# Turning gated features by VectorE and by way of memory, in a two-layer decoder trunk

## The chip, the cores and the metric

The kernel runs on one core of a Trainium2 chip. The metric is the device time of one execution in microseconds (us), lower is better. A core has several engines that run their own instruction streams in order and meet through semaphores: TensorE (PE, matrix products into PSUM; PEld is its loading of the stationary operand), VectorE (DVE), ScalarE (ACT), GpSimd (POOL) and SyncE (SP, which here only issues DMA transfers).

## The reference, cut to what matters

256 tokens, a model width of 1024, two layers. Each layer has a gated feed-forward block (FFN), a mixing block with two kinds of attention, a second FFN, and a per-layer embedding gate; so there are four FFNs, named a0, b0, a1 and b1 here (first and second FFN of layer 0 and of layer 1). All is float32.

```python
D_FF = 2816
def swiglu(x, w_gate, w_up, w_down):
    return (jax.nn.silu(x @ w_gate) * (x @ w_up)) @ w_down
...
    h = h + 0.5 * swiglu(rms_norm(h, ffn1_norm), ffn1_w_gate, ffn1_w_up, ffn1_w_down)
...
    h = h + 0.5 * swiglu(rms_norm(h, ffn2_norm), ffn2_w_gate, ffn2_w_up, ffn2_w_down)
```

The change concerns the tensor between the two halves of `swiglu`: the gated features, 256 tokens by 2816 features.

## The kernel before, in words

**Number form.** A float32 product is made of three products of a reduced form: every operand is split into a rounded high part and the rest (`wh` and `wl` for weights, `fh` and `fl` for gated features). ACT writes the high part (a copy that rounds), DVE subtracts it from the whole. `mm3` (L241) then issues three matmuls: high by high (L243), and two mixed ones, of which L244 reads `wl`.

**Weights.** A weight piece is 128 partitions by 1024 numbers (512 KB). SP loads it into one of 7 buffers `raw`, ACT makes `wh` (L139), DVE makes `wl` (L140); there are 8 buffers of each, so the splitting can be at most 8 pieces ahead of the product. Some blocks use seven products in place of eight (`Seven`, L161): there DVE also forms sums of raw weight pieces (L175), splits at L181, and ACT rounds at L180.

**FFN.** The 2816 features are worked in blocks of 512 (five) and one of 256, by `ffn` (L508). For a plain block the gate product `g` and the up product `u` are made for two halves of tokens (128 tokens each, t = 0 and 1), tokens on partitions: eight weight pieces. A block in `wide_sevens` is made by `wide_seven` (L547): first seven products of four weight pieces, then four more pieces. In a0 that is block 3 alone, in the other FFNs blocks 1 and 3. Then `gated` (L511) makes silu on ACT (`s`, L513) and the gated product on DVE (`pr`, L517), tokens on partitions.

**Turning.** The second half of the FFN needs the features on the partitions. `Gates.add` (L479) defers it: `go` has TensorE transpose the 128x512 tile in four 128x128 pieces into a PSUM bank (`ft`, L488), ACT rounds it into `fh` (L493) and DVE subtracts into `fl` (L494). For blocks 1, 2 and 3 `sums` (L435) also forms four sums of turned quarters, with an ACT copy (L451) and four subtractions or additions on DVE (L452 to L455), and splits them (L459, L460, L463, L464).

**Order.** `soon` (L222) puts a deferred piece into the program after so many us of estimated PE time, `flush` (L233) puts in all that are left. A scheduler then sets the order of each engine's instructions from its own estimates; each engine runs its list strictly in that order. SP's loads, ACT's roundings and DVE's splits of later weights are thus placed among the work on `pr`, `fh` and `fl`. Small work tiles come from tags `w0` to `w3` with two buffers each.

Of the kernel before, what the change touches and what calls it, by code (L numbers as in the profile page):

```python
# [9 lines left out]
F32 = mybir.dt.float32  # L10
# [7 lines left out]
P = 128  # L18
T = 256
# [33 lines left out]
def trunk(ctx: ExitStack, tc: tile.TileContext, xT, xr, pT, w, gains, fgain, consts, out):  # L53
# [218 lines left out]
    def wt(tag, name, n=2, width=T):  # L272

        return tp.tile([P, 768], F32, tag=tag, name=name)[:, : n * width].rearrange("p (a b) -> p a b", a=n)
# [4 lines left out]
    def half(f):  # L279
        return slice(f * 512, (f + 1) * 512)  # L280


    def split(x, src, c, gcol, name, ts=slice(0, T)):

# [130 lines left out]
    class Gates:  # L415
# [19 lines left out]
        def sums(self, i):  # L435

            a, b = self.turned[i, 0], self.turned[i, 1]
            lo, hi = slice(0, 2), slice(2, 4)
            e = SEVEN.index(i)
            if e == 0:  # L440

                self.spare = tuple(x_p.tile([P, KC, T], F32R, tag=f"x{q}", name=f"sx{q}_{self.tag}") for q in "hl")
            if e < 2:
                homes = [[q[:, 4 * e + k].rearrange("p (a b) -> p a b", a=2) for q in self.spare] for k in range(4)]
            else:

                homes = [[q[:, 2 + k].rearrange("p (a b) -> p a b", a=2) for q in self.tile(NBLK - 1)] for k in range(2)]
                homes += [[q[:, lo, P:T] for q in self.tile(b)] for b in SEVEN[:2]]
            two = [wt(f"w{2 + k}", f"sum{k}_{self.tag}_{i}") for k in range(2)]
            ss = s1, s2, s3, s4 = [two[k // 2][:, k % 2].rearrange("p (a b) -> p a b", a=2) for k in range(4)]  # L450
            nc.scalar.copy(s3, b[:, lo])  # L451
            nc.vector.tensor_tensor(s1, s3, b[:, hi], ALU.subtract)  # L452
            nc.vector.tensor_tensor(s2, s1, a[:, lo], ALU.subtract)
            nc.vector.tensor_tensor(s3, a[:, lo], s3, ALU.subtract)
            nc.vector.tensor_tensor(s4, s2, a[:, hi], ALU.add)  # L455
            if e < 2:
                for k in range(2):
                    sh, sl = (q[:, 4 * e + 2 * k : 4 * e + 2 * k + 2] for q in self.spare)
                    nc.scalar.activation(sh, two[k], AF.Copy)  # L459
                    nc.vector.tensor_tensor(sl, two[k], sh.bitcast(F32), ALU.subtract)  # L460
            else:
                for k, (sh, sl) in zip(ss, homes):
                    nc.scalar.activation(sh, k, AF.Copy)  # L463
                    nc.vector.tensor_tensor(sl, k, sh.bitcast(F32), ALU.subtract)  # L464
            self.s[i] = homes
# [12 lines left out]

        def add(self, i, t, pr, more):  # L479

            f = self.block(i)
            n = 4 if i < NBLK - 1 else 2

            def go():
                a = bank(f"ft_{self.tag}_{i}{t}")[:, : n * P]
                behind = newest_mm[0]
                for j in range(n):
                    after(nc.tensor.transpose(a[:, j * P : (j + 1) * P], pr[:, j * P : (j + 1) * P], ident), behind)  # L488
                a = a.rearrange("p (a b) -> p a b", a=n)

                ks = slice(2 if i in SEVEN and t else 0, n)
                fh, fl = both(f, slice(None), ks, slice(t * P, (t + 1) * P))
                nc.scalar.activation(fh, a[:, ks], AF.Copy)  # L493
                nc.vector.tensor_tensor(fl, a[:, ks], fh.bitcast(F32), ALU.subtract)  # L494
                self.turned[i, t] = a
                if i in SEVEN and t:
                    self.sums(i)

            soon(1.3 + 0.9 * t + more, go)

    def seven_mm(banks, x_of, ops, first, last):

# [5 lines left out]
    def ffn(x, n, tag, gcol, between=None, feed=None):  # L508
# [15 lines left out]
        def x_sums():  # L524

            v = f_p.tile([P, 4, T], F32, tag="f5h", name=f"xf_{tag}")
            xh, xl = (q[:, 0:4].bitcast(F32) for q in x)
            nc.vector.tensor_tensor(v, xh, xl, ALU.add)
            a11, a12, a21, a22 = (v[:, k : k + 2, t * P : (t + 1) * P] for t in range(2) for k in (0, 2))
            two = [wt(f"w{2 + k}", f"xsum{k}_{tag}") for k in range(2)]  # L530
            s1, s2, s3, s4 = (two[k // 2][:, k % 2].rearrange("p (a b) -> p a b", a=2) for k in range(4))
            nc.vector.tensor_tensor(s1, a21, a22, ALU.subtract)
            nc.vector.tensor_tensor(s2, s1, a11, ALU.subtract)
            nc.vector.tensor_tensor(s3, a11, a21, ALU.subtract)
            nc.vector.tensor_tensor(s4, s2, a12, ALU.add)
            xs.extend(f_p.tile([P, 4, T], F32R, tag=f"f4{q}", name=f"xs{q}_{tag}") for q in "hl")
            for k in range(2):
                sh, sl = (q[:, 2 * k : 2 * k + 2] for q in xs)
                nc.scalar.activation(sh, two[k], AF.Copy)
                nc.vector.tensor_tensor(sl, two[k], sh.bitcast(F32), ALU.subtract)  # L540
# [105 lines left out]

        head, tail = block(0), block(NBLK - 1)
        plain(head[:2], True)
        flush()

        p = {2: d[0][0], 3: d[0][1], 4: d[1][0]}
        p.update((i, bank(f"p{i}_{tag}")) for i in (1, 5, 6, 7))
        own = (1, 5, 6, 7)
        for i, c in zip(SEVEN, (head[2:], tail, [])):
            seven_mm(p, gates.seven(i), Seven().operands(), lambda q: q in own and i == SEVEN[0], lambda q: q in own and i == SEVEN[-1])
            plain(c)
            if i == SEVEN[1] and between is not None:
                between()
# [420 lines left out]
def _weights(i):  # L1079
# [9 lines left out]
    for L in range(DEPTH):  # L1089
# [5 lines left out]
        def ffn(n):  # L1095
            wg, wu, wd = (i[f"{n}_w_{s}"][L] for s in ("gate", "up", "down"))
            for j in range(NBLK - 1):
                m = ar(512 * j, 512 * j + 512)
                if j in wide_sevens(L == 0 and n == "ffn1"):
                    units.extend(np.concatenate([cols(v[k : k + 256], m) for v in (wg, wu)], axis=1) for k in (0, 256))  # L1100
                    units.extend(cols(v[512:], m) for v in (wg, wu))
                    continue
                wide(wg, m)
                wide(wu, m)
            m = ar(DFF - 256, DFF)
            wide(np.concatenate([wg[:, m], wu[:, m]], axis=1), ar(512))

            def down(b):
                units.extend(cols(wd[k : k + 256], ar(DM)) for k in range(512 * b, min(512 * b + 512, DFF), 256))

            def seven(b):
                for k in (512 * b, 512 * b + 256):
                    units.append(np.concatenate([cols(wd[k : k + 256], ar(c, c + 512)) for c in (0, 512)], axis=1))

            down(0)
            down(NBLK - 1)
            for b in SEVEN:
                seven(b)
            down(4)
# [81 lines left out]
```

## Time and profile before

| what | value |
|---|---|
| median of 3 executions | 1011.65 us (1010.78 to 1012.71) |
| profiled execution: time | 1010.68 us |
| profiled execution: span from first to last instruction | 1008.9 us |
| PE busy | 996.9 us (99%) |
| DVE busy | 839.9 us (83%) |
| ACT busy | 645.7 us (64%) |
| TensorE clock granted (mean) | 0.997 |
| DMA, mean over the span | 186 GB/s, 187.40 MB |

Times in rows are us from the start of the span unless they stand in a column of ns. The profile names tiles without their numbers: `wl` is any low part of a weight piece, `ft_a` a turned tile of a0 or a1, `ft_b` one of b0 or b1. `L488` is line 488 of the kernel. A matmul's row shows its whole passage, of which the next one's overlaps a part: how long PE is held by it is read from one start to the next. The same holds on DVE, where a row's time is a little longer than the step to the next start.

### The profile page before, as it was taken

To read this page: it belongs to the slowest core of one execution; us is meant where nothing else is said; L and a number is where in the kernel's file an instruction comes from. 1 tells how busy PE (TensorE), PEld (TensorE's weight loads), DVE (VectorE), ACT (ScalarE), POOL (GpSimd) and SP (SyncE) were. 2 spreads that over 40 slices of the span, in tenths; PEclk is the share of its full clock that TensorE was granted. 3 is DMA by queue.
4 is the path that set the end of the run, shared out by engine and by line. 5 is a ranking of instruction groups with operands and counts; after the bars stand their busy time and mean duration, and the time that the engine had idled before them with its cause. 6 is when DMAs were issued, how large, how long until landed. Compare 5 with 4: busy or idle time off the path is not lost.

```text
span 1008.9 us, 13852 instructions
## 1 busy us (share of the span) xinstructions
PE 996.9 (99%) x5064; PEld 842.3 (83%) x5064; DVE 839.9 (83%) x1170; ACT 645.7 (64%) x986; POOL 7.4 (1%) x13
## 2 busy tenths in 40 slices
PE   9999999999999999999999999999999999999996
PEld 8888888899888888888887888889998888888885
DVE  5799789966779987899998887899676898978994
ACT  5856566667566665657775665656766675656663
POOL 0000000000100000000000000000010000000000
PEclk9999999999999999999999999999999999999998
DMA  8947446674244566356637464557623364744641
GB/s 293 334 185 273 140 152 228 221 250 152 84 147 136 198 197 242 127 176 233 231 130 252 147 229 135 185 191 262 238 84 126 105 203 185 240 165 146 205 161 42
DMA packets 53492, 187.40 MB, mean 186 GB/s; under 512 B 6064, under 2 KB 6192, under 8 KB 53424
## 3 DMA queue, kind: packets, MB, share of 16 engines
q1 hardware_dynamic: 52992, 185.95, 54.1%
q8 instruction: 39, 0.64, 0.2%
q10 hardware_dynamic: 432, 0.57, 0.2%
q14 instruction: 29, 0.24, 0.1%
HBM read 185.45 MB, written 1.05 MB: 185 GB/s over the span
## 4 chain that ended last, share of the span: by engine, by line
PE 96%; ACT 1%; DVE 1%; DMA 1%; issue 1%; POOL 0%; DVEq 0%; ACTq 0%; POOLq 0%
PE p_b L243 3%; PE p_b L245 3%; PE p_b L244 3%; PE g_a L243 3%; PE g_a L245 3%; PE g_a L244 3%; PE g_b L245 3%; PE g_b L243 3%; PE g_b L244 3%; PE d_b L245 3%; PE d_b L244 3%; PE d_b L243 3%; PE u_a L244 3%; PE u_a L245 3%; PE u_a L243 3%; PE d_a L244 3%
## 5 line engine op out<-in xcount | busy, mean ns | idle before, releaser
L140 DVE TENSOR_TENSOR wl<-raw,wh 128x1024 fp32r<-128x1024 f32 (+1 forms) x278 | 324.5, 1191 | 59.3 <-ACT wh L139 58.8
L139 ACT ACTIVATE wh<-raw 128x1024 fp32r<-128x1024 f32 (+1 forms) x278 | 282.8, 1035 | 120.3 <-DMA raw<-in_w 14.4
L180 ACT ACTIVATE wh<-raw 128x1024 fp32r<-128x1024 f32 x133 | 139.6, 1060 | 123.2 <-DVE raw L175 58.7
L181 DVE TENSOR_TENSOR wl<-raw,wh 128x1024 fp32r<-128x1024 f32 x133 | 159.3, 1220 | 24.4 <-ACT wh L180 23.6
L175 DVE TENSOR_TENSOR raw<-raw,raw 128x1024 f32<-128x1024 f32 x76 | 92.7, 1219 | 14.9 <-DMA raw<-in_w 13.2
L243 PE MATMUL d_a<-wh,fh_a 128*128 128x512 f32 x108 | 42.7, 396 | 0.0
L243 PE MATMUL d_b<-wh,fh_b 128*128 128x512 f32 x108 | 42.7, 396 | 0.0
L245 PE MATMUL d_b<-wh,fl_b 128*128 128x512 f32 x108 | 42.1, 390 | 0.0
L245 PE MATMUL d_a<-wh,fl_a 128*128 128x512 f32 x108 | 42.1, 390 | 0.0
L244 PE MATMUL d_a<-wl,fh_a 128*128 128x512 f32 x108 | 42.1, 389 | 0.0
L244 PE MATMUL d_b<-wl,fh_b 128*128 128x512 f32 x108 | 42.1, 389 | 0.0
L243 PE MATMUL g_a<-wh,x0h 128*128 128x512 f32 x80 | 31.9, 401 | 0.0
L245 PE MATMUL g_a<-wh,x0l 128*128 128x512 f32 x80 | 31.0, 390 | 0.0
L244 PE MATMUL g_a<-wl,x0h 128*128 128x512 f32 x80 | 31.0, 390 | 0.0
L243 PE MATMUL g_b<-wh,x_mix0h 128*128 128x512 f32 x64 | 25.6, 400 | 0.0
L243 PE MATMUL g_b<-wh,x_mix1h 128*128 128x512 f32 x64 | 25.6, 400 | 0.0
L243 PE MATMUL g_a<-wh,xe0h 128*128 128x512 f32 x64 | 25.5, 401 | 0.0
L245 PE MATMUL g_a<-wh,xe0l 128*128 128x512 f32 x64 | 25.1, 392 | 0.0
L244 PE MATMUL u_a<-wl,x0h 128*128 128x512 f32 x64 | 25.0, 391 | 0.0
L245 PE MATMUL g_b<-wh,x_mix0l 128*128 128x512 f32 x64 | 25.0, 390 | 0.0
L245 PE MATMUL g_b<-wh,x_mix1l 128*128 128x512 f32 x64 | 25.0, 390 | 0.0
L244 PE MATMUL g_a<-wl,xe0h 128*128 128x512 f32 x64 | 25.0, 390 | 0.0
(556 smaller groups left out, 2702.2 us busy)
## 6 DMA issues: line engine op xcount, KB each, us to landing
raw<-in_w SPq DMA_DIRECT2D x338, 512.0 KB, 4.6
raw<-in_w SPq DMA_DIRECT2D x16, 256.0 KB, 4.6
xin<-in_xT SPq DMA_DIRECT2D x4, 256.0 KB, 5.1
h<-in_xr SPq DMA_DIRECT2D x2, 512.0 KB, 8.5
p<-in_pT SPq DMA_DIRECT2D x2, 256.0 KB, 4.8
fg<-in_fgain SPq DMA_DIRECT2D x1, 512.0 KB, 5.2
out_h<-hg SPq DMA_DIRECT2D x2, 256.0 KB, 2.3
out_h<-hg ACTq DMA_DIRECT2D x2, 256.0 KB, 2.7
```

The costliest lines, as they stand in the source:

```text
L139: nc.scalar.activation(wh[:, a], r[:, a], AF.Copy),
L140: nc.vector.tensor_tensor(wl[:, a], r[:, a], wh[:, a].bitcast(F32), ALU.subtract),
L175: nc.vector.tensor_tensor(self.raw[o], self.raw[a], self.raw[b], op)
L180: newest_wh[0] = nc.scalar.activation(wh, r, AF.Copy)
L181: nc.vector.tensor_tensor(wl, r, wh.bitcast(F32), ALU.subtract)
L243: nc.tensor.matmul(o, ah, bh, start=start, stop=False, **kw)
L244: nc.tensor.matmul(o, ah, bl, start=False, stop=False, **kw)
L245: newest_mm[0] = nc.tensor.matmul(o, al, bh, start=False, stop=stop, **kw)
```

## The change

The gated product `pr` is turned by one DVE instruction, in place, in blocks of 32 by 32 (tokens by features within each block). The turned tile is written to a buffer in memory (`m`, one DMA on SP), and four more DMAs on SP bring it back, 32 partitions each, so that every partition holds all tokens of its features (`ft`, now in a `w2` tile in SBUF, no longer in PSUM). Two estimates, `BACK` and `PARTS`, say when the DMAs back and the splitting stand in the program. The weight columns of gate and up are stored in another order, so that each feature lands on the partition that the down weights expect. In `sums` the ACT copy is gone (both sources are in SBUF), and its tiles come from `w3` alone. The first `flush` in the second half of the FFN stands behind the first seven products.

```diff
+BACK, PARTS = 2.5, 7.0
+def turned_order(n):
+    import numpy as np
+    return np.arange(n).reshape(n // P, 4, 32).transpose(1, 0, 2).reshape(-1)
...
+    mem_p = pool("mem", 4, space=bass.MemoryType.DRAM)
...
+    def in_runs(x):
+        return x.rearrange("p j (a s) -> p j a s", s=32)
...
-            two = [wt(f"w{2 + k}", f"sum{k}_{self.tag}_{i}") for k in range(2)]
-            ss = s1, s2, s3, s4 = [two[k // 2][:, k % 2].rearrange("p (a b) -> p a b", a=2) for k in range(4)]
-            nc.scalar.copy(s3, b[:, lo])
-            nc.vector.tensor_tensor(s1, s3, b[:, hi], ALU.subtract)
-            nc.vector.tensor_tensor(s2, s1, a[:, lo], ALU.subtract)
-            nc.vector.tensor_tensor(s3, a[:, lo], s3, ALU.subtract)
-            nc.vector.tensor_tensor(s4, s2, a[:, hi], ALU.add)
+            two = [wt("w3", f"sum{k}_{self.tag}_{i}") for k in range(2)]
+            ss = [two[k // 2][:, k % 2].rearrange("p (a b) -> p a b", a=2) for k in range(4)]
+            s1, s2, s3, s4 = (in_runs(s) for s in ss)
+            nc.vector.tensor_tensor(s1, b[lo], b[hi], ALU.subtract)
+            nc.vector.tensor_tensor(s2, s1, a[lo], ALU.subtract)
+            nc.vector.tensor_tensor(s3, a[lo], b[lo], ALU.subtract)
+            nc.vector.tensor_tensor(s4, s2, a[hi], ALU.add)
...
-            def go():
-                a = bank(f"ft_{self.tag}_{i}{t}")[:, : n * P]
-                behind = newest_mm[0]
-                for j in range(n):
-                    after(nc.tensor.transpose(a[:, j * P : (j + 1) * P], pr[:, j * P : (j + 1) * P], ident), behind)
-                a = a.rearrange("p (a b) -> p a b", a=n)
+            name = f"{self.tag}_{i}{t}"
+            nc.vector.transpose(pr, pr)
+            m = mem_p.tile([P, 4, n * 32], F32, tag="turn", name=f"m_{name}")
+            nc.sync.dma_start(m, pr.rearrange("p (q r) -> p q r", q=4))
+            a = wt("w2", f"ft_{name}", 4, n * 32)
+
+            def back():
+                for q in range(4):
+                    nc.sync.dma_start(a[32 * q : 32 * q + 32], m[:, q].rearrange("(a f) r -> f a r", a=4))
+
+            def parts():
+                self.turned[i, t] = v = a.rearrange("p a (j s) -> p j a s", j=n)
...
-                fh, fl = both(f, slice(None), ks, slice(t * P, (t + 1) * P))
-                nc.scalar.activation(fh, a[:, ks], AF.Copy)
-                nc.vector.tensor_tensor(fl, a[:, ks], fh.bitcast(F32), ALU.subtract)
-                self.turned[i, t] = a
+                fh, fl = (in_runs(q) for q in both(f, slice(None), ks, slice(t * P, (t + 1) * P)))
+                after(nc.scalar.activation(fh, v[:, ks], AF.Copy), newest_wh[0])
+                nc.vector.tensor_tensor(fl, v[:, ks], fh.bitcast(F32), ALU.subtract)
...
-            soon(1.3 + 0.9 * t + more, go)
+            soon(BACK, back)
+            soon(PARTS + t, parts)
...
-            two = [wt(f"w{2 + k}", f"xsum{k}_{tag}") for k in range(2)]
+            two = [wt("w3", f"xsum{k}_{tag}") for k in range(2)]
...
         plain(head[:2], True)
-        flush()
...
             seven_mm(p, gates.seven(i), Seven().operands(), lambda q: q in own and i == SEVEN[0], lambda q: q in own and i == SEVEN[-1])
+            flush()
...
-                m = ar(512 * j, 512 * j + 512)
+                m = 512 * j + turned_order(512)
...
-            m = ar(DFF - 256, DFF)
+            m = DFF - 256 + turned_order(256)
```

The order of instructions moves with it. On DVE in a0, at the end of block 2 (`pr_a0_20`, `pr_a0_21`) and the start of the wide block 3 (`raw7_12` and `wl7_12` are its four raw pieces and their splits; `wl14` is the first piece behind its seven products, `wl11` the last unit of block 2), the list before is:

```order
L181 TENSOR_TENSOR wl7_12_1_33_751<-raw7_12_1_745,wh7_12_1_33_750 128x1024
L540 TENSOR_TENSOR xsl_a0_714<-xsum1_a0_708,xsh_a0_713 128x512
L175 TENSOR_TENSOR raw7_12_0_725<-raw7_12_0_725,raw7_12_1_745 128x1024
L175 TENSOR_TENSOR raw7_12_1_745<-raw7_12_0_725,raw7_12_3_747 128x1024
L181 TENSOR_TENSOR wl7_12_0_34_780<-raw7_12_0_725,wh7_12_0_34_779 128x1024
L181 TENSOR_TENSOR wl7_12_1_35_793<-raw7_12_1_745,wh7_12_1_35_792 128x1024
L181 TENSOR_TENSOR wl7_12_2_36_806<-raw7_12_2_803,wh7_12_2_36_805 128x1024
L175 TENSOR_TENSOR raw7_12_0_725<-raw7_12_0_725,raw7_12_2_803 128x1024
L181 TENSOR_TENSOR wl7_12_0_37_817<-raw7_12_0_725,wh7_12_0_37_816 128x1024
L517 SCALAR_TENSOR_TENSOR pr_a0_20_699<-u_a0_20_522,hr_in_102,s_a0_20_623 128x512
L517 SCALAR_TENSOR_TENSOR pr_a0_21_703<-u_a0_21_523,hr_in_102,s_a0_21_625 128x512
L181 TENSOR_TENSOR wl7_12_3_38_827<-raw7_12_3_747,wh7_12_3_38_826 128x1024
```

And after the change, at the same place on DVE (two rows for the turning stand behind the gated products):

```order
L188 TENSOR_TENSOR raw7_12_1_759<-raw7_12_1_759,raw7_12_3_761 128x1024
L540 SCALAR_TENSOR_TENSOR pr_a0_20_712<-u_a0_20_538,hr_in_104,s_a0_20_636 128x512
L540 SCALAR_TENSOR_TENSOR pr_a0_21_720<-u_a0_21_539,hr_in_104,s_a0_21_638 128x512
L502 STREAM_TRANSPOSE pr_a0_20_712<-pr_a0_20_712 128x512
L502 STREAM_TRANSPOSE pr_a0_21_720<-pr_a0_21_720 128x512
L194 TENSOR_TENSOR wl7_12_1_33_765<-raw7_12_1_759,wh7_12_1_33_764 128x1024
L188 TENSOR_TENSOR raw7_12_0_746<-raw7_12_0_746,raw7_12_1_759 128x1024
L188 TENSOR_TENSOR raw7_12_1_759<-raw7_12_0_746,raw7_12_3_761 128x1024
L194 TENSOR_TENSOR wl7_12_0_34_784<-raw7_12_0_746,wh7_12_0_34_783 128x1024
L194 TENSOR_TENSOR wl7_12_1_35_797<-raw7_12_1_759,wh7_12_1_35_796 128x1024
L194 TENSOR_TENSOR wl7_12_2_36_810<-raw7_12_2_807,wh7_12_2_36_809 128x1024
```

Before, five of the seven splits stood ahead of the gated products of block 2; now one does, and the rest stands behind them. From `pr_a0_20` to the split of `wl14_0` the list now holds 10 instructions of 128x1024 (that split among them), 2 gated products, 2 turnings, 5 others of 128x512 and 5 of 128x256; before it held 2 of 128x1024, 2 gated products and 1 other of 128x512.

On SP in a0, the first block (`m_a0_00` and `m_a0_01` are the tiles in memory of the two token halves, `ft` the tiles that are brought back, the rest weight pieces), the list after is:

```order
L148 DMA raw8_0_0_24_542<-in_w 128x1024
L504 DMA m_a0_00_423<-pr_a0_00_418 128x512
L504 DMA m_a0_01_431<-pr_a0_01_428 128x512
L148 DMA raw8_1_0_25_568<-in_w 128x1024
L509 DMA ft_a0_00_425<-m_a0_00_423 32x4x128 x4
L509 DMA ft_a0_01_433<-m_a0_01_431 32x4x128 x4
L148 DMA raw9_0_0_26_586<-in_w 128x1024
L148 DMA raw9_1_0_27_620<-in_w 128x1024
L148 DMA raw10_0_0_28_642<-in_w 128x1024
L504 DMA m_a0_10_527<-pr_a0_10_522 128x512
L504 DMA m_a0_11_533<-pr_a0_11_530 128x512
L148 DMA raw10_1_0_29_660<-in_w 128x1024
```

Before, the same list held the weight pieces alone. Now the load of `raw8_1` stands behind two writes that wait for DVE, and that of `raw9_0` behind eight DMAs that wait for those writes to land.

## Rows read from the trace of the kernel before

**Rows 1.** The page: busy time by engine, with share of the span and instructions, and shares of the chain of work that ended last.

```profile
PE 996.9 (99%) x5064; PEld 842.3 (83%) x5064; DVE 839.9 (83%) x1170; ACT 645.7 (64%) x986; POOL 7.4 (1%) x13
...
PE 96%; ACT 1%; DVE 1%; DMA 1%; issue 1%; POOL 0%; DVEq 0%; ACTq 0%; POOLq 0%
```

**Rows 2.** Who waited for whom, PE alone: us in total, times, longest.

```profile
PE ft_a L488 <- DVE pr_a L517: 1.5, 1, 1.5
```

**Rows 3.** Windows over the four FFNs (a0, b0, a1, b1; each from its first product to near its last): length, then busy us of PE, PEld, DVE, ACT and POOL with the number of instructions, granted clock, DMA share, GB/s.

```profile
5.00:182.00 177.00, 177.00 (x802) 146.07 (x802) 150.82 (x189) 114.53 (x155) 0.00 (x0) 1.00 0.66 229
290.00:467.00 177.00, 177.00 (x808) 146.45 (x807) 155.89 (x195) 110.85 (x146) 0.00 (x0) 1.00 0.54 186
508.00:679.00 171.00, 169.53 (x768) 139.82 (x768) 147.38 (x177) 104.19 (x128) 0.00 (x0) 1.00 0.54 182
788.00:965.00 177.00, 177.00 (x807) 146.44 (x806) 155.98 (x196) 110.75 (x145) 0.00 (x0) 1.00 0.55 186
```

**Rows 4.** The transposes: the groups by source line (durations in ns), and PE's timeline around one group of four and one of two (start, time, instruction; in a start-to-start step PE is held).

```profile
L488 PE MATMUL ft_a<-c_sb,pr_a x88: 270/272/299, 45.3 to 630.2; 128*128 128x128 f32 x88
L488 PE MATMUL ft_b<-c_sb,pr_b x88: 270/272/273, 317.5 to 916.9; 128*128 128x128 f32 x88
...
45.08 0.39 PE L245 MATMUL u_a<-wh,x0l 128*128 128x512 f32 x1
45.31 0.60 PE L488 MATMUL ft_a<-c_sb,pr_a 128*128 128x128 f32 x4
45.67 0.47 PE L243 MATMUL u_a<-wh,x0h 128*128 128x512 f32 x1
45.98 0.39 PE L244 MATMUL u_a<-wl,x0h 128*128 128x512 f32 x1
...
417.41 0.38 PE L488 MATMUL ft_b<-c_sb,pr_b 128*128 128x128 f32 x2
417.54 0.48 PE L243 MATMUL d_b<-wh,fh_b 128*128 128x512 f32 x1
417.86 0.40 PE L244 MATMUL d_b<-wl,fh_b 128*128 128x512 f32 x1
```

**Rows 5.** DVE instructions from SBUF to SBUF, by source line (ns, smallest, median, largest): one source of 512 elements; and the groups by form of two sources, 512 and 1024 elements (busy us, mean ns).

```profile
L830 DVE TENSOR_SCALAR on_mla<-os,tss_mla x4: 480/486/489, 278.4 to 776.5; 128x512 f32<-128x512 f32 x4
...
L460 DVE TENSOR_TENSOR sxl_a<-sum_a,sxh_a 128x512 fp32r<-128x512 f32 x8 | 5.2, 686 | 0.2 <-ACT sxh_a L459 0.2
L140 DVE TENSOR_TENSOR wl<-raw,wh 128x1024 fp32r<-128x1024 f32 x262 | 314.1, 1222 | 53.0 <-ACT wh L139 52.5
```

**Rows 6.** DMA issues: size of one, and median us from issue to landing. The row of 64 KB is 128 runs of 512 bytes.

```profile
raw<-in_w SPq DMA_DIRECT2D x338, 512.0 KB, 4.6
out_h<-hg SPq DMA_DIRECT2D x2, 256.0 KB, 2.3
c_sb<-in_consts SPq DMA_DIRECT2D x1, 64.0 KB, 4.0
```

**Rows 7.** SP's timeline: issues at the start of a0 and before block 3.

```profile
18.25 0.44 SPq L1050 DMA_DIRECT2D h<-in_xr  x1
40.36 4.32 SPq L135 DMA_DIRECT2D raw<-in_w  x4
```

**Rows 8.** Timelines of DVE and PE in a0, block 0's gated products, the split behind them, and the first matmul that reads that split.

```profile
36.45 1.41 DVE L517 SCALAR_TENSOR_TENSOR pr_a<-u_a,hr_in,s_a 128x512 f32<-128x512 f32 x2 [1.46 <-ACT s_a L513]
37.98 1.23 DVE L140 TENSOR_TENSOR wl<-raw,wh 128x1024 fp32r<-128x1024 f32 x1
39.38 0.40 PE L244 MATMUL u_a<-wl,x0h 128*128 128x512 f32 x1
```

**Rows 9.** Timelines in a0 from block 1's gated products to block 3's first plain piece: DVE, then PE's first matmul that reads `wl14_0`.

```profile
51.12 1.40 DVE L517 SCALAR_TENSOR_TENSOR pr_a<-u_a,hr_in,s_a 128x512 f32<-128x512 f32 x2
...
64.43 2.48 DVE L175 TENSOR_TENSOR raw<-raw,raw 128x1024 f32<-128x1024 f32 x2
66.84 3.62 DVE L181 TENSOR_TENSOR wl<-raw,wh 128x1024 fp32r<-128x1024 f32 x3
...
73.94 1.41 DVE L517 SCALAR_TENSOR_TENSOR pr_a<-u_a,hr_in,s_a 128x512 f32<-128x512 f32 x2
...
81.56 0.42 DVE L454 TENSOR_TENSOR sum_a<-ft_a,sum_a 128x256 f32<-128x256 f32 x1
81.89 0.41 DVE L455 TENSOR_TENSOR sum_a<-sum_a,ft_a 128x256 f32<-128x256 f32 x1
83.07 0.39 PE L244 MATMUL p_a<-wl,x0h 128*128 128x512 f32 x1
```

**Rows 10.** Timelines in b0 at the first wide block: DVE's gated products of block 0 and what follows, and PE's first matmul that reads the first plain piece of block 1, whose split is the row at 320.18.

```profile
315.94 1.40 DVE L517 SCALAR_TENSOR_TENSOR pr_b<-u_b,hr_mix,s_b 128x512 f32<-128x512 f32 x2
317.26 2.35 DVE L181 TENSOR_TENSOR wl<-raw,wh 128x1024 fp32r<-128x1024 f32 x2
319.52 0.68 DVE L494 TENSOR_TENSOR fl_b<-ft_b,fh_b 128x512 fp32r<-128x512 f32 x1
320.18 1.23 DVE L140 TENSOR_TENSOR wl<-raw,wh 128x1024 fp32r<-128x1024 f32 x1
324.08 0.39 PE L244 MATMUL p_b<-wl,x_mix0h 128*128 128x512 f32 x1
```

**Rows 11.** PE's timeline in a1 where PE waits (in brackets the idle time and what ended it).

```profile
551.21 0.63 PE L488 MATMUL ft_a<-c_sb,pr_a 128*128 128x128 f32 x4 [1.47 <-DVE pr_a L517]
```

More of the change, by code (lines that the diff above doesn't have):

```diff
@@ L437, in sums @@
             a, b = self.turned[i, 0], self.turned[i, 1]
-            lo, hi = slice(0, 2), slice(2, 4)
+            lo, hi = (slice(None), slice(0, 2)), (slice(None), slice(2, 4))
             e = SEVEN.index(i)
@@ L447, in sums @@
                 homes = [[q[:, 2 + k].rearrange("p (a b) -> p a b", a=2) for q in self.tile(NBLK - 1)] for k in range(2)]
-                homes += [[q[:, lo, P:T] for q in self.tile(b)] for b in SEVEN[:2]]
-            two = [wt(f"w{2 + k}", f"sum{k}_{self.tag}_{i}") for k in range(2)]
-            ss = s1, s2, s3, s4 = [two[k // 2][:, k % 2].rearrange("p (a b) -> p a b", a=2) for k in range(4)]
-            nc.scalar.copy(s3, b[:, lo])
-            nc.vector.tensor_tensor(s1, s3, b[:, hi], ALU.subtract)
-            nc.vector.tensor_tensor(s2, s1, a[:, lo], ALU.subtract)
-            nc.vector.tensor_tensor(s3, a[:, lo], s3, ALU.subtract)
-            nc.vector.tensor_tensor(s4, s2, a[:, hi], ALU.add)
+                homes += [[q[:, 0:2, P:T] for q in self.tile(c)] for c in SEVEN[:2]]
+            two = [wt("w3", f"sum{k}_{self.tag}_{i}") for k in range(2)]
[5 more added lines that the diff above has]
+            nc.vector.tensor_tensor(s4, s2, a[hi], ALU.add)
             if e < 2:
```

## Prediction

> **What bounds the kernel now.** I read the page first. PE is busy for 996.9 of 1008.9 us and the chain of work that ended last is PE for 96% [rows 1]; the reader is to see that an instruction taken off PE shortens the run by its own hold, as long as nothing makes PE wait instead. The list of PE's waits shows one that matters, 1.5 us [rows 2]. So all other engines are hidden, and the question is how well. The windows over the four FFNs say that: DVE is busy for 150.8 of 177, 155.9 of 177, 147.4 of 171 and 156.0 of 177 us [rows 3], that is 85 to 88%. The change gives DVE more to do there. Last I read timelines at places where PE reads a split piece soon after DVE has made it [rows 8 to 10], since an average cannot tell whether a piece comes in time.
>
> **What is removed from PE.** 88 transposes in `ft_a` and 88 in `ft_b` [rows 4]: per FFN ten groups of four and two groups of two, so 40 groups of four and 8 of two. The duration of one, 272 ns, is its passage and not its hold. By starts: the matmul at 45.08 is followed by the transposes at 45.31 (a step of 0.23), and two matmuls later PE is at 45.98, where without the group it would be at 45.31 + 0.23 = 45.54. A group of four holds PE for 0.44 to 0.45 us. The group of two starts at 417.41, and the second matmul behind it at 417.86, against 417.64: 0.22 us. Sum: 40 x 0.45 + 8 x 0.22 = 19.8 us. The Trainium skill, "VectorE: DVE Perf Modes", section "The three transpose paths", gives TensorE 390 ns for one 128x128 transpose (bf16) and VectorE 311; by that the 176 would be worth 68.6 us and the run would end near 942. The trace has 0.11 us of hold for one, so the measurement decides and the sum does not use it.
>
> The wait of 1.47 us at 551.21 is PE standing at a transpose whose `pr_a` DVE had not yet made [rows 2, 11]. PE has no such instruction any more, and what stands behind it needs no `pr`: 1.5 us more. Together 21.3 us are to be had, and the time with nothing given back is 1010.68 - 21.3 = 989.4.
>
> **What is added.** *DVE:* 40 turnings of 128x512 and 8 of 128x256. No row shows one. From below the nearest row is a one-source instruction from SBUF to SBUF of 512 elements, 0.49 us; from above the split of 1024 elements, 1.22, as if every element took two steps; the two-source 512 takes 0.69 [rows 5]. Starts come some 0.07 before the end of the one in front (1.41 for two of 0.74 in [rows 8]), so as steps 0.42, 1.15 and 0.62. I take 0.62, a step for an element as in the middle row. Per FFN that is 10 x 0.62 + 2 x 0.35 = 6.9 us, and DVE would stand at 158 to 163 of some 172 us (PE's 177 less 4.9): 92 to 95%, not full. The splits `fl` and the sums read SBUF where they read PSUM; their counterparts with SBUF sources cost the same 0.69 [rows 5], so nothing. *ACT* loses a copy per block with sums and is 62 to 65% busy [rows 3]: nothing. *DMA:* one write of 256 KB and four reads of 64 KB per tile, some 23 MB against 187, while the queues are busy for 54 to 66% in the FFNs [rows 3]: no bound by volume.
>
> *SP:* a write of `m` waits for the turning, and the weight loads behind it wait too; the four reads wait for the write to land, and the loads behind them wait again. An issue takes 0.44 us free and 1.08 in a loaded stretch [rows 7]. A write of 256 KB lands in 2.3, a read of 64 KB in runs of 512 bytes in 4.0, a load of 512 KB in 4.6 [rows 6]. A round trip is thus about 0.4 + 2.3 + 4 x 0.44 + 3 to 4 = 7.5 to 8.5 us for one tile, the second token half 2 us later; with the loaded issue and 4.6 for each landing it is 14. The skill's same section warns that a plain DMA that does a transpose by strides is 19 times slower than the transposing DMA; the row of 64 KB, which has the very runs of the reads back (512 bytes), landed in 4.0 us [rows 6], so I do not count on that.
>
> **Where cover ends: a0.** The lists in the section on the change differ most there, and this is the term that decides.
>
> First, `wl6_0` (the split at 37.98) ends at 39.21 and PE reads it at 39.38 [rows 8]. Two turnings now stand in front of it: 1.24 less the margin of 0.17 to 0.2 is 1.0 us of waiting.
>
> Second, the wide block 3. Before, DVE had made five of its seven splits when block 2's gated products came at 73.94 [rows 9]. The new list puts one split before them and the rest behind, and PE cannot end block 2 sooner than it does, so the chain is fixed by the order: from `pr_a0_20` to the end of `wl14_0` DVE has 10 of 1024 elements (a step of 1.2, from 64.43 to 66.84 for two), 2 gated products (0.67), 2 turnings (0.62), 5 of 512 (0.61) and 5 of 256 (0.34, from 81.56 to 81.89) [rows 9]: 12.0 + 1.3 + 1.2 + 3.1 + 1.7 = 19.3 us. PE did that stretch in 83.07 - 73.94 = 9.1 us, now 8.2 without its two groups of transposes. It waits 11.1 us, spread over the seven products.
>
> Third, DVE reaches `pr_a0_20` a little late. From `pr_a0_10` (51.12 before [rows 9], now about 51.2: less two groups of transposes, 0.9, plus the 1.0 above) the list has 18.7 us of steps up to `pr_a0_20`, but `fl` of block 1 stands in it 7.9 us behind `pr_a0_10`, and the round trip that starts at 53.8 brings the first half back at 62 and the second at 64: some 4 us of waiting. That gives 73.9; PE has block 2 ready at 73.9 - 1.8 + 1.0 = 73.1. I count 0.8.
>
> From `wl14_0` on DVE needs 1.2 per piece and PE 2.7 (twelve matmuls of 0.23), so the lead comes back and nothing of the loss is made good.
>
> **The other FFNs.** There the wide block 1 follows block 0 in both versions and the list keeps its order; only the turnings come in. At 315.94 in b0: 1.3 for two products, 1.2 for two turnings, 2.3 for two splits, 0.6 for one sum of products that now stands ahead, 1.15 for the split: 322.5. PE reads it at 324.08 less two groups, 323.2 [rows 10]. 0.7 us are left, so no wait; a1 and b1 have the same lists. A turning of 1.15 would use up 1.06 more and cost 0.4 in each. Where `fl` used to stand in that stretch it now comes later, when the tile is back: by the same steps DVE reaches it 11.3 us behind 315.94, 9.3 behind the end of the first turning, against a round trip of 7.5 to 8.5. It just fits. Late in each FFN (blocks 4 and 5, and the down products) no piece depends on the trip for many products, and I count nothing.
>
> **Sum**, against the profiled execution: 1010.68 - 19.8 - 1.5 + 1.0 + 11.1 + 0.8 = 1002.3. That execution lies 0.97 below the median of the runs, so I take 1003.
>
> **Bounds.** A turning of 0.42 takes 0.2 off each of four in a0 and of two in the late term: 1001. One of 1.15 adds 0.5 x 4 there, 1 us to the late term and 0.4 x 3 in the others: 1007 to 1008. A trip of 14 us adds 6 to the late term in a0: 1009; both, 1013 or more. Below, if the order cost nothing in a0, 989.4. So the likeliest case has 999 to 1007 for itself.
>
> **Rivals.**
> - *The whole gain comes, 990.* For it: PE is the bound and DVE has 5% left on average. Against it: lists are run in order, and the 19.3 us in a0 are made of DVE steps alone. It needs DVE steps half as long. 0.10.
> - *The cover is used up everywhere, 1008 to 1013.* The turning takes two steps for an element, or the trip is near 14 us; each by itself leaves 2 to 3 us of gain. For it: DVE at 95% and a margin of 0.7 us in three FFNs. Against it: the row of 0.69. 0.14.
> - *Slower, 1020 (1014 to 1035).* One mechanism: ACT's rounding `fh` waits for the tile from memory, and ACT's weight roundings stand behind it in its list. With a trip of T us the splits in each wide block start T - 9 us late. As long as that is below PE's lead it is hidden; past it every us is PE's. The three later FFNs have two wide blocks each, so with a trip of 14 and 2 us of lead it is 3 x 6 = 18 us, on top of 1002: 1020. It decides from where each of the six loses 1.9 us, a trip of about 13. For it: loads of 512 KB stand in the same queues, and their landing takes 4.6 at the median. Against it: the rows of 2.3 and 4.0. 0.14.
>
> That the change leaves PE's transposes in place is excluded by the list of instructions.
>
> **Chances and range.** Likeliest case 0.62, the whole gain 0.10, cover used up 0.14, slower 0.14. What a measurement of this kernel can tell from no change is about 0.2%, 2 us: faster is below 1009.6, slower above 1013.7. Faster: 0.62 + 0.10 + a third of 0.14 = 0.77; the same: 0.09; slower: 0.14. The range from 996 to 1012 leaves out the whole gain, most of the slower case and some of the third.
>
> **What would show it.** PE's rows without L488, and PE busy some 20 us less with idle time of some 12 us, nearly all between 38 and 95 us, waiting for `wl` of DVE. `wl14_0` read near 94 instead of 83. In b0, a1 and b1 no PE wait above 1 us. The turning near 0.69 us. From a write's issue to the last landing of `ft` 8 to 10 us. I am wrong in the main step if PE does not wait in a0 (then the time is near 990), or if waits of ACT for `ft` grow in the later FFNs and PE idles there.

## The result, and the profile after

The changed kernel takes 1005.62 us (median of 5 runs, 1003.63 to 1007.24) against 1011.08 (5 runs, 1010.56 to 1012.71). The ratio is 0.9943, with a 95% interval from 0.9927 to 0.9958. The profiled execution took 1003.63 with a span of 1001.8, which is 2 us under the median of its kernel.

The page of the changed kernel, busy times and shares of the chain; they answer to [rows 1].

```profile
PE 981.6 (98%) x4888; PEld 824.2 (82%) x4888; DVE 861.9 (86%) x1218; ACT 635.7 (63%) x974; POOL 12.4 (1%) x13
...
PE 86%; DVE 5%; DMA 4%; ACT 3%; issue 1%; SPq 0%; ACTq 0%; DVEq 0%
```

PE has 176 instructions less. Its busy time fell by 15.3 us and its idle time rose from 12.0 to 20.2. DVE and DMAs now stand in the chain. What PE waited for (us in total, times, longest), against the single row of [rows 2]:

```profile
PE p_a L257 <- DVE wl L194: 3.8, 3, 2.0
PE e L257 <- DVE wl L153: 1.7, 1, 1.7
PE p_a L256 <- ACT wh L193: 1.6, 2, 1.1
PE pv L257 <- DVE wl L153: 1.4, 2, 0.8
...
PE u_a L257 <- DVE wl L153: 0.5, 1, 0.5
```

`p_a` are the products of the wide block in a0. `pv` and `e` lie behind b0 and b1, where the forecast had no wait. The windows over the four FFNs, and one of 5 us in a0 (columns as in [rows 3]):

```profile
5.00:190.00 185.00, 178.61 (x774) 144.31 (x774) 160.43 (x210) 116.46 (x160) 0.00 (x0) 0.99 0.74 253
285.00:460.00 175.00, 175.00 (x782) 144.54 (x781) 157.93 (x206) 108.07 (x149) 0.00 (x0) 1.00 0.64 210
500.00:670.00 170.00, 170.00 (x755) 140.49 (x754) 156.77 (x196) 107.16 (x137) 0.00 (x0) 1.00 0.66 217
780.00:960.00 180.00, 180.00 (x802) 148.59 (x801) 164.40 (x212) 112.02 (x151) 0.00 (x0) 1.00 0.65 218
...
75.00:80.00 5.00, 3.11 (x7) 1.81 (x7) 4.93 (x6) 2.19 (x3) 0.00 (x0) 0.66 0.49 169
```

PE is never idle in b0, a1 and b1, with DVE at 90 to 92%. In a0 it is. The timelines of the wide block in a0, DVE first, then PE (start, time, instruction, and in brackets the idle time with what ended it); [rows 9] has the same place before.

```profile
72.65 1.40 DVE L540 SCALAR_TENSOR_TENSOR pr_a<-u_a,hr_in,s_a 128x512 f32<-128x512 f32 x2
73.97 1.29 DVE L502 STREAM_TRANSPOSE pr_a<-pr_a 128x512 f32<-128x512 f32 x2
75.19 1.18 DVE L194 TENSOR_TENSOR wl<-raw,wh 128x1024 fp32r<-128x1024 f32 x1
76.30 2.47 DVE L188 TENSOR_TENSOR raw<-raw,raw 128x1024 f32<-128x1024 f32 x2
78.69 3.62 DVE L194 TENSOR_TENSOR wl<-raw,wh 128x1024 fp32r<-128x1024 f32 x3
...
90.50 1.22 DVE L153 TENSOR_TENSOR wl<-raw,wh 128x1024 fp32r<-128x1024 f32 x1
...
76.42 0.80 PE L257 MATMUL p_a<-wl,xsh_a 128*128 128x512 f32 x1 [1.98 <-DVE wl L194]
91.77 0.50 PE L257 MATMUL p_a<-wl,x0h 128*128 128x512 f32 x1 [0.19 <-DVE wl L153]
```

DVE has no gap from 72.65 to 90.50. Six of the seven splits of the wide block stand behind `pr_a0_20` here, where before six stood ahead of it and one behind (not five ahead, as the section on the change and the prediction have it). The row at 90.50 is the split of `wl14_0`, and PE reads it at 91.77, 19.1 us behind `pr_a0_20`; before, 9.1.

SP's issues 10 to 20 us earlier, and what ACT and DVE then waited for:

```profile
51.94 1.14 SPq L504 DMA_DIRECT2D m_a<-pr_a  x2
53.19 0.38 SPq L148 DMA_DIRECT2D raw<-in_w  x1
54.02 5.59 SPq L509 DMA_DIRECT2D ft_a<-m_a  x8
59.66 0.91 SPq L148 DMA_DIRECT2D raw<-in_w  x2
60.61 1.89 SPq L185 DMA_DIRECT2D raw<-in_w  x4
...
59.40 1.06 ACT L152 ACTIVATE wh<-raw 128x1024 fp32r<-128x1024 f32 x1 [8.35 <-DMA raw<-in_w]
...
60.49 1.23 DVE L153 TENSOR_TENSOR wl<-raw,wh 128x1024 fp32r<-128x1024 f32 x1 [4.60 <-ACT wh L152]
```

SP stood at the write of `m_a0_10` until DVE had turned the tile, then at the reads until the write had landed. The loads of the wide block (L185) went out from 60.61 on; before, from 45.49 on.

The page's list of DMA issues (size, median us to landing), and the turning by form:

```profile
m_a<-pr_a SPq DMA_DIRECT2D x20, 256.0 KB, 2.1
ft_a<-m_a SPq DMA_DIRECT2D x80, 64.0 KB, 2.7
...
L502 DVE STREAM_TRANSPOSE pr_b<-pr_b 128x512 f32<-128x512 f32 x20 | 13.0, 685 | 0.0
```

**Where the time went.** For every matmul that both programs have, the difference of its starts in the two traces was taken. It is flat over long stretches and moves at a few places, so it can be read stage by stage (us, minus is earlier; the last column is the difference at the last matmul). The rows below the first are experiments told further on, against the same trace of before.

| kernel | first products | a0 | b0 | behind b0 | a1 | behind a1 | b1 | behind b1 | all |
|---|---|---|---|---|---|---|---|---|---|
| the change | -0.6 | +5.1 | -5.1 | +3.3 | -7.2 | +1.5 | -5.1 | +1.3 | -6.7 |
| e2, no trip | -0.7 | -2.3 | -5.2 | 0.0 | -7.2 | +0.2 | -5.3 | 0.0 | -20.6 |
| e3, no turning | -0.5 | +3.9 | -5.1 | +3.4 | -6.6 | +1.2 | -5.2 | +1.7 | -7.2 |
| e4, a0 on PE | -0.4 | +0.5 | -5.0 | +3.1 | -7.2 | +2.7 | -5.1 | +1.4 | -10.0 |
| e5, writes on ACT | -0.2 | +5.4 | -5.2 | +0.5 | -7.2 | +0.4 | -5.2 | 0.0 | -11.5 |
| e8, both of these | -0.2 | +0.8 | -5.2 | +0.1 | -7.2 | +0.6 | -5.2 | 0.0 | -16.3 |
| e11, e5 with another list in a0 | +0.1 | +0.2 | -5.2 | 0.0 | -7.1 | +0.1 | -5.2 | 0.0 | -16.9 |

Each later FFN gains 5.1 us, a1 another 2.1. a0 gives back its 5.05 and 5.09 more, 10.1 in all, and 6.1 us go behind the three later FFNs.

### The profile page after: what moved, and what is told of

Its sections match the earlier page's. It is cut to its first block, busy times and chain, and to the rows that moved or that the text cites. A ratio compares the mean times of both kernels' runs of the same rounds, so it can differ in the third digit from the quotient of the medians.

```text
span 1001.8 us, 14087 instructions
## 1 busy us (share of the span) xinstructions
PE 981.6 (98%) x4888; PEld 824.2 (82%) x4888; DVE 861.9 (86%) x1218; ACT 635.7 (63%) x974; POOL 12.4 (1%) x13
## 4 chain that ended last, share of the span: by engine, by line
PE 86%; DVE 5%; DMA 4%; ACT 3%; issue 1%; SPq 0%; ACTq 0%; DVEq 0%
DMA raw<-in_w 4%; PE p_b L256 3%; PE g_a L256 3%; PE p_b L257 3%; PE g_a L258 3%; PE g_a L257 3%; PE g_b L257 3%; PE g_b L258 3%; PE g_b L256 3%; PE p_b L258 3%; PE d_a L257 3%; PE d_a L258 3%; PE d_a L256 3%; PE p_a L257 3%; PE p_a L258 3%; PE p_a L256 2%
## 5 line engine op out<-in xcount | busy, mean ns | idle before, releaser
L153 DVE TENSOR_TENSOR wl<-raw,wh 128x1024 fp32r<-128x1024 f32 (+1 forms) x278 | 321.0, 1187 | 49.5 <-ACT wh L152 48.1
L152 ACT ACTIVATE wh<-raw 128x1024 fp32r<-128x1024 f32 (+1 forms) x278 | 278.5, 1031 | 103.2 <-DMA raw<-in_w 47.4
L194 DVE TENSOR_TENSOR wl<-raw,wh 128x1024 fp32r<-128x1024 f32 x133 | 159.4, 1216 | 11.1 <-ACT wh L193 10.4
L258 PE MATMUL u_a<-wh,x0l 128*128 128x512 f32 x64 | 25.0, 390 | 0.0
```

The source lines that it names most:

```text
L152: nc.scalar.activation(wh[:, a], r[:, a], AF.Copy),
L153: nc.vector.tensor_tensor(wl[:, a], r[:, a], wh[:, a].bitcast(F32), ALU.subtract),
L194: nc.vector.tensor_tensor(wl, r, wh.bitcast(F32), ALU.subtract)
L258: newest_mm[0] = nc.tensor.matmul(o, al, bh, start=False, stop=stop, **kw)
```

## The experiments

Three theories stood at the start. S: SP's list, in which weight loads stand behind the trip. V: DVE's added work. L: the length of the trip, at whose end ACT's `fh` waits with weight roundings behind it. A fourth, O, came with the results: the written order of DVE's list in a0. Medians, and ratios to the kernel before on the same chip:

| run | median us | ratio, 95% interval |
|---|---|---|
| e1_trip_on_pool | 1054.79 | 1.0444 (1.0429 to 1.0460) |
| e2_no_trip | 989.94 | 0.9795 (0.9780 to 0.9810) |
| e3_no_turning | 1005.27 | 0.9945 (0.9930 to 0.9960) |
| e4_a0_on_pe | 1000.06 | 0.9895 (0.9878 to 0.9911) |
| e5_write_on_act | 997.50 | 0.9863 (0.9849 to 0.9878) |
| e6_trip_on_act | 1098.37 | 1.0863 (1.0841 to 1.0886) |
| e7_pool_late_fh | 1011.36 | 1.0002 (0.9990 to 1.0014) |
| e8_a0_pe_write_act | 993.70 | 0.9826 (0.9811 to 0.9840) |
| e9_a0_reads_on_act | 1004.76 | 0.9934 (0.9919 to 0.9948) |
| e10_a0_reads_on_pool | 1000.14 | 0.9886 (0.9869 to 0.9902) |
| e11_a0_list | 993.39 | 0.9824 (0.9810 to 0.9837) |
| e12_a0_list_sp | 1008.05 | 0.9966 (0.9952 to 0.9979) |

**e2 and e3: trip or turning.**

```diff
-            m = mem_p.tile(...)
-            nc.sync.dma_start(m, ...)
-            a = wt("w2", f"ft_{name}", 4, n * 32)
+            a = pr.rearrange("p (a r) -> p a r", a=4)
...
-            soon(BACK, back)
```

> The trip through memory is left out: no writes, no reads back, and fh, fl and the sums read the turned tile itself, so that features lie on the wrong partitions and the output is not the reference's. The turnings stay. Theory S and theory L: about 989 (987 to 992), the whole gain. Theory V: 1000 to 1006, since DVE's list has every instruction that it had.

```diff
-            nc.vector.transpose(pr, pr)
```

> The 48 turnings on DVE are left out and the trip stays, so the output is not the reference's. DVE has 6.9 us less to do in each FFN. Theory S: the loads stand behind the trip as before; the order of DVE's list in a0 still has the splits behind pr_a0_20, and the time is 1000 to 1004, 1 to 5 us less than the 1005.6 of the change, from turnings no longer in front of late splits. Theory V: nearly the whole gain, 989 to 993. Theory L: 1002 to 1006.

Without the trip nearly the whole gain came: 989.94, against 989.4 in the forecast for nothing given back. (In the table a0 still gives back some 2.7 us, -2.3 where 5.05 are taken off; other stages gain more than was counted.) PE's largest wait and DVE's busiest window in that kernel:

```profile
PE p_a L257 <- DVE wl L153: 1.2, 1, 1.2
...
780.00:960.00 180.00, 180.00 (x804) 149.13 (x803) 169.98 (x226) 114.61 (x158) 0.00 (x0) 1.00 0.54 189
```

DVE does all its turnings, is busy for 94% of b1's window, and PE never waits there. Without the turnings but with the trip, the time is that of the change (1005.27, above what S had and inside L's range). V falls as the main cause: the turnings cost 1 to 3 us, all in a0 (e3 gives back 1.2 us less there than the change, e2 still 2.7), and leaving the trip out saves 15 to 16 us.

**e1, e6, e7: the trip issued elsewhere.** The edit of e1; in e6 it is `nc.scalar`:

```diff
-            nc.sync.dma_start(m, ...)
+            nc.gpsimd.dma_start(m, ...)
...
-                    nc.sync.dma_start(a[32 * q : 32 * q + 32], ...)
+                    nc.gpsimd.dma_start(a[32 * q : 32 * q + 32], ...)
```

> The 48 writes and 192 reads of the trip through memory are issued by POOL instead of SP; nothing else is changed. In the changed kernel SP's weight loads stand behind these DMAs, in a0 the first load of the wide block goes out at 60.6 us instead of 45.5. Theory S (what is given back, 10.0 us in a0 and 3.3, 1.5 and 1.3 us in the stages behind b0, a1 and b1, comes from weight loads held up on SP): the loads are early again, the splits stand ahead of pr_a0_20, and the time falls from 1005.6 to about 990 (988 to 994). Theory V (DVE has too much to do, the turnings above all, wherever the DMAs are issued): 1002 to 1006, as now. Theory L (the trip itself is too long for fh and fl, from whatever queue): 1000 to 1010, with longer waits of ACT for ft. The turning 0.67 us in each.

> Writes and reads back are all issued by ACT (240 DMAs, some 0.4 us each: 24 us of ACT's time in each FFN, so 106 to 116 of 170 us become 130 to 140). SP has weight loads alone, in the order of the kernel before. Theory S: no PE wait from late loads; 989 to 994, unless ACT's waiting for turnings and landings makes the roundings late. Theory L: as long as it waits in order, 1000 to 1020 with PE waiting for wh and wl; it is then ACT's list that is held up, by fh and by the DMAs.

e1 took 1054.79, which no theory had. Its DMA issues, ACT's waits, and PE's largest wait:

```profile
m_a<-pr_a POOLq DMA_DIRECT2D x20, 256.0 KB, 2.9
ft_a<-m_a POOLq DMA_DIRECT2D x80, 64.0 KB, 5.5
...
ACT fh_b L516 <- DMA ft_b<-m_b: 54.3, 14, 8.2
ACT fh_a L516 <- DMA ft_a<-m_a: 51.0, 14, 11.6
...
PE p_b L257 <- DVE wl L194: 9.3, 9, 2.6
```

ACT stood at `fh` for 105 us, 6.3 in the change (3.1 and 3.2). This is the wait of theory L, in a kernel with a longer trip: from a write's issue to the last landing of its tile the median is 11.5 us instead of 6.8, a read takes 5.5 us to land instead of 2.7, and its issue 0.55 instead of 0.42. In e6 ACT waits for `ft` for 183 us, and PE waits mostly for `wh`; the 1098.37 lie far above what L had too. In both, SP has the weight loads alone, as S asked for, and its gain did not come. e7 tests the reading of e1:

```diff
-BACK, PARTS = 2.5, 7.0
+BACK, PARTS = 2.5, 30.0
```

> As e1_trip_on_pool (1054.8 us), with the splitting of the tile that comes back asked for 30 us of TensorE time after the turning instead of 7, which puts fh a few roundings further back in ACT's list. If e1 is long because ACT stands at fh until a trip of 12 to 14 us has ended, with the weight roundings behind it, this takes a good part of the 65 us away: 1000 to 1030. If it is long because of POOL's DMAs themselves (slow descriptors, contention with the loads), it stays at 1045 to 1060.

e7 took 1011.36 us: 43 of the 65 us are gone with the DMAs still on POOL. ACT's waits for `ft` fell to 70 us. So it was mainly where `fh` stands in ACT's list, not POOL's DMAs as such.

**e4 and e5: where, and which wait.** In e4 the code of before is kept beside the new one and taken in a0:

```diff
+ON_PE = ("a0",)
...
+            if self.tag in ON_PE:
+                soon(1.3 + 0.9 * t + more, go)
+                return
             nc.vector.transpose(pr, pr)
```

In e5:

```diff
-            nc.sync.dma_start(m, pr.rearrange("p (q r) -> p q r", q=4))
+            nc.scalar.dma_start(m, pr.rearrange("p (q r) -> p q r", q=4))
```

> The first FFN, a0, is as in the kernel before (transposes on TensorE, weight columns in plain order); the three others are changed. All theories: a0 loses the 10.0 us that it gives back and the 4.95 us that it gains, so 5.0 less than the change: about 1000.5 (999 to 1002). What is left of the loss is behind b0, a1 and b1: waits of PE of about 1.7 us behind b0. If the time stays at 1004 or above, the losses behind the FFNs are larger than the one in a0, and the place named for the loss is wrong.

> Only the 48 writes of the trip are issued by ACT; the 192 reads back stay on SP. SP then has no DMA that waits for a turning; the reads, which wait for the write to land, stand further back in its list (in a0 the loads of raw8_1 to raw11_1 now go before them or between). Theory S in the form that it is the wait for the turning that holds the loads up: 989 to 994. Theory S in the form that eight reads in a row on SP (some 4 us of issuing and a wait for the landing) hold them up as well: 995 to 1002. Theory L: 1000 or more. ACT waits for a turning 24 times at most, at places where it has weight roundings in hand; if that hurts, PE waits for wh of ACT.

e4 gained 5.6 us, about as expected, and kept the losses behind the FFNs (7.2 us in the table). e5 did the reverse. PE's waits in e5:

```profile
PE p_a L257 <- DVE wl L194: 4.0, 3, 2.2
PE p_a L256 <- ACT wh L193: 1.2, 2, 0.7
```

No wait for `pv` and `e` is left, and the 6.1 us behind b0, a1 and b1 are 0.9 in the table. The only edit is the queue of the writes; the lists that follow from it keep the weight loads in the same order. So there S holds: SP's writes held the weight loads up. SP at the end of b0, first in the change, then in the kernel before, then in e5:

```profile
406.75 0.92 SPq L504 DMA_DIRECT2D m_b<-pr_b  x2
407.76 0.51 SPq L185 DMA_DIRECT2D raw<-in_w  x1
409.38 4.16 SPq L509 DMA_DIRECT2D ft_b<-m_b  x8
413.65 0.84 SPq L148 DMA_DIRECT2D raw<-in_w  x2
419.81 0.81 SPq L504 DMA_DIRECT2D m_b<-pr_b  x2
420.71 0.40 SPq L185 DMA_DIRECT2D raw<-in_w  x1
421.60 3.92 SPq L509 DMA_DIRECT2D ft_b<-m_b  x8
425.57 1.38 SPq L185 DMA_DIRECT2D raw<-in_w  x3
```

```profile
401.72 19.32 SPq L172 DMA_DIRECT2D raw<-in_w  x4
```

```profile
404.05 0.33 SPq L185 DMA_DIRECT2D raw<-in_w  x1
410.17 3.66 SPq L509 DMA_DIRECT2D ft_b<-m_b  x8
413.92 7.49 SPq L185 DMA_DIRECT2D raw<-in_w  x3
```

Counted through from the start, the four loads that went out from 401.72 on before are the one at 420.71 and the three from 425.57 on in the change, and the one at 404.05 and the three from 413.92 on in e5. Most of DVE's last splits of b0 then come 3 to 4.5 us later than before, those of the next weights 6 to 8, and PE's lead of some 5 us is used up. That a load lands in 5.1 us instead of 4.6 (medians) is not the reason: in e5 it takes 5.1 too.

As a whole, 997.50 lies in the range that S had for its second form, in which the eight reads on SP hold the loads up as well. For in a0 e5 changed nothing: there the loads of the wide block still went out from 60.56 on, behind eight reads. The runs from e9 on take that up.

**e8: the edits of e4 and e5 together.**

> a0 as in the kernel before (transposes on TensorE), the three other FFNs changed with the writes on ACT as in e5_write_on_act (997.5). e5 gives back some 10 us in a0 and gains 4.95 there, and has no wait behind b0, a1 and b1; so 5 us less than e5, 992 to 993, if the three FFNs are independent of a0; from the whole gain of e2_no_trip, 989.9, plus 4.95 for a0: 994.9. Expected 992 to 996. Above 997 would mean that what is lost in a0 is not lost in its wide block.

e8 took 993.70 us, inside the expected range.

**e9 to e12: a0.** e9 and e10 issue eight reads elsewhere:

```diff
-                    nc.sync.dma_start(a[32 * q : 32 * q + 32], ...)
+                    (nc.scalar if self.tag == "a0" and i == 1 else nc.sync).dma_start(a[32 * q : 32 * q + 32], ...)
```

> As e5_write_on_act (997.5), and the eight reads back of a0's block 1 are issued by ACT too. The four loads of the wide block 3 then stand in SP's list right behind raw11_1, with no wait for a landing ahead: issued near 47 to 52 us instead of 60.6. DVE's list still has six of the seven splits behind pr_a0_20: by its steps 18 us up to wl14_0 against PE's 8.2. Theory O (in a0 the written order of DVE's list decides, wherever the loads are): PE waits some 10 us in the wide block as in e5, 996 to 999. Theory S (the late loads decide): the wait is gone, 988 to 991.

> As e9, with these eight reads on POOL. DVE's list now has two more splits and one more sum ahead of pr_a0_20; from there to wl14_0 it holds 2 gated products, 2 turnings, 7 instructions of 1024 elements and 5 of 512: 1.3 + 1.2 + 8.4 + 3.0 = 13.9 us against PE's 8.2. Theory O: PE waits 5 to 6 us in a0 instead of 10, so 992 to 994. Theory S: 988 to 991. Theory L (POOL's longer trip of 12 to 14 us holds fh, and wh behind it, in ACT's list): 996 or more.

Then the list itself was changed, with the writes on ACT (e11) or SP (e12):

```diff
+                    if late:
+                        after(d, newest_load[0])
...
-            soon(BACK, back)
-            soon(PARTS + t, parts)
+            late = self.tag == "a0" and i in (1, 2)
+            soon(32 if late else BACK, back)
+            soon((36 if late else PARTS) + t, parts)
```

> As e5_write_on_act (997.5), and in a0 the reads back of blocks 1 and 2 and the splitting of what they bring stand 32 and 36 us of TensorE time behind the turning (2.5 and 7 before), behind the newest weight load. The instructions and their queues are those of e5; only the lists change: on DVE five of the seven splits of the wide block 3 again stand ahead of pr_a0_20, and from there to wl14_0 are 2 gated products, 2 turnings, 3 of 1024 elements and 1 of 512: 1.3 + 1.2 + 3.6 + 0.6 = 6.7 us against PE's 8.2. Theory O (the written order behind the trip is what a0 gives back): the 10 us of a0 are gone, 988 to 991, faster than the kernel before by some 21 us and than e8 by some 4. If it stays at 996 or above, the order in a0 is not the cause.

> The change (1005.6) with the same later reads and splitting in a0 as e11, but the writes stay on SP. Stages behind b0, a1 and b1 as in the change: they give back their 6.1 us. In a0, DVE's list from pr_a0_20 to wl14_0 is 2 gated products, 2 turnings, 6 of 1024, 3 of 512 and 1 of 256: 1.3 + 1.2 + 7.2 + 1.8 + 0.3 = 11.8 us against 8.2, a wait of 3 to 4 us instead of 8 to 10. Theory O: 998 to 1001. If SP's writes that wait for the turning make the loads late in a0 beyond that, 1001 to 1004; no change, 1005, would speak for the late loads alone.

No whole time fell where O had put it: e9 and e10 came out 6 us above, e11 2 and e12 7. But the stretch that O speaks of, from `pr_a0_20` to PE's reading of `wl14_0`, was foreseen (us; the sum of DVE's steps in the written list, put down before, and the trace):

| kernel | list | trace |
|---|---|---|
| the change | 19.3 | 72.65 to 91.77: 19.1 |
| e9 | 18 | 79.52 to 98.85: 19.3 |
| e10 | 13.9 | 81.05 to 95.19: 14.1 |
| e12 | 11.8 | 71.39 to 83.40: 12.0 |
| e11 | 6.7 (PE alone 8.2) | 71.39 to 78.90: 7.5 |

In e9 two of the four loads went out earlier, at 50.72 and 54.73, the other two at 60.79 and 61.21, hardly earlier than in the change. But the last had landed at 66.91, 12.6 us ahead of `pr_a0_20` (1.4 in the change), and the stretch stayed the same. (Five of the seven splits stood behind `pr_a0_20` in e9, not six.) In e11 the list was right too, and the wait was gone (lines of the gated product stand 3 further down):

```profile
71.39 1.43 DVE L543 SCALAR_TENSOR_TENSOR pr_a<-u_a,hr_in,s_a 128x512 f32<-128x512 f32 x2 [0.69 <-PE u_a L258]
72.74 1.29 DVE L502 STREAM_TRANSPOSE pr_a<-pr_a 128x512 f32<-128x512 f32 x2
73.96 2.32 DVE L194 TENSOR_TENSOR wl<-raw,wh 128x1024 fp32r<-128x1024 f32 x2
...
78.90 0.39 PE L257 MATMUL p_a<-wl,x0h 128*128 128x512 f32 x1
```

So O holds for the wide block of a0: the written order sets its length, not the time at which its weights arrive. The misses are waits that a move made elsewhere. In e9 ACT stands at `fh` (6.81 us at 61.95) with the weights of block 2 behind it, and PE waits 4.8 us for `wl` in `u_a`. In e10 PE waits 6.6 us for `xsh_a`, which stands behind `fh` in ACT's list, as L said. In e11 and e12 the difference to before stands at -3.7 and -2.0 us at 100 us, +5.9 in the change; then they lose some 5 and 10 us in the rest of a0, where block 2's tile is fetched only behind block 3's, from 107.87 and 108.91 us on. In e12 most of this falls between 135 and 145 us, where the difference goes from -3.4 to +3.3: PE stands 3.3 us at `wh` of the seven products (2.5 at once, at 139.89), and the granted clock is 0.66 from 140 to 145. In e11 the loss is spread out, and was not taken apart.

e8 and e11, 993.70 and 993.39, beat both kernels and cannot be told from one another. The 989.94 of e2 was not reached by a kernel that brings the features to their places.

## Why the prediction was right

The forecast was 1003, the median 1005.62, inside the range of 996 to 1012 and on the side of 0.77. The working holds in most steps, and one step failed. Its size was partly made up by what was put too high in a0 and by gains that were not counted, so that the number came this near is in part luck.

- *Transposes, 19.8 us.* The three later FFNs gain 5.1 each, 20.2 for four: right. So the hold read from starts was the thing to price, not the passage of 272 ns. The wait of 1.5 us in a1 is gone with 0.6 more.
- *The turning.* It took 0.685 us with a step of 0.60 (1.29 for two); 0.69 and 0.62 were taken. The page of the Trainium skill, "VectorE: DVE Perf Modes", section "The three transpose paths", warns of plain DMAs that transpose by strides, where the innermost stride of the destination is large. The reads back write runs of 512 bytes and landed in 2.7 us, so the trace gives no sign of that here.
- *The round trip, 7.5 to 8.5 us.* This was put a little too long. In a0's block 0 the writes go out at 37.46 and 38.05 and the last reads of the two tiles land at 44.15 and 45.17: 6.7 and 7.1 us. Over the 48 tiles it is 6.8 at the median (5.3 to 9.3). The 14 us of the bounds rest on a misreading of [rows 7]: the four loads there take 0.33 us each to issue and start 1.1 to 1.7 us apart, each as SP's wait for a split by DVE ends (40.36 behind the one that ends at 40.34); 1.08 us is not the time of an issue.
- *`wl6_0`, 1.0 us.* The gated products came 1.0 us earlier (35.41 against 36.45 in [rows 8]), and 0.2 was lost.
- *The wide block, 11.1 us.* The list's 19.3 us came out as 19.1. a0 as a whole gave back 10.1 where the three terms made 12.9; PE's own list had drawn nine products (2.0 us) ahead of the reading of `wl14_0`, so part of the wait was filled.
- *The late term, 0.8 us.* About 0.8 at 70 us, by another way: DVE stood 4.60 us at a split whose weights SP had sent late, not at `fl`. This is the step that failed below, at work in a0 already.
- *"Late in each FFN ... no piece depends on the trip for many products, and I count nothing."* This step failed. It looked at pieces that depend on the trip, and left out those that only stand behind it on SP. They cost 6.1 us behind b0, a1 and b1, and e5 gives 5 of these back. It is the order of weight loads on SP, which the prediction names under *SP* and then puts no price on.

The sum of what was seen: 20.2 + 2.1 + 0.6 gained, 10.1 + 6.1 given back, 6.7 at the last matmul and 7.1 in the span (1008.9 to 1001.8). The forecast's sum of 1002.3 stands against 1003.63 for the profiled execution: 2.8 us too much in a0, 6.1 missing behind the others, and 2.0 more gained elsewhere than counted.

Of the rivals, the whole gain is what e2 shows to be possible, by a way that the forecast did not name: DVE needs no faster steps, only another order. The slower rival's mechanism is real. It decided from a trip of about 13 us. In e1, from a write's issue to the last landing, it is 11.5 us at the median (6.7 to 16.5); in a0's block 0 the turnings end at 38.69 and 39.28 and `fh` starts at 50.64 and 53.10. The price of 18 us was far too small: e1 loses 49 us to the change.

## What to carry to other kernels

Here, work that moved from the bound engine to one with some 6% left (b1 in e2) was free in three FFNs of four; a wait in the queue of the weight loads was not. Before moving a step through memory, list for each of its DMAs what stands behind it on that queue, not only what needs its data, and look where the planner has put the urgent work of the engine that takes the step over. A written list's steps, summed between two events, gave that stretch within 1.3 us four times; in e11 the list was short enough that PE set the stretch.

## What was not expected of the hardware

- Reads of 64 KB landed in 2.7 to 2.9 us when SP issued them (the change) and in 5.5 to 6.1 when POOL did (e1), with an issue of 0.42 and 0.55 us. The Trainium skill, "DMA: Bandwidth & Descriptors", section "SWDGE vs HWDGE vs iDMA", calls the path that SP and ACT use the one with the faster setup. The same eight reads agree: from ACT in e9 they landed in 2.8 us, from POOL in e10 in 8.0 (medians). But the issuing engine is not all of it: when ACT issued all 192 (e6) they took 5.1 to 5.3 us, with an issue of 0.44. Why was not taken apart.
- After PE's wait of 1.98 us in a0 the granted clock had a mean of 0.66 in the window from 75 to 80 us, and from 77.02 matmuls followed each other by 0.43 us instead of 0.23, the lower level of 1.2 GHz. From 80.32 on the step is 0.23 again. It probably cost nothing here, since DVE ran its list without a gap; no run tests that.
